# Gate and up loop of a two-layer trunk: where loads and sums for the down projection are written

## The chip, the cores and the metric

The kernel runs on one core of one Trainium2 chip. The metric is the time of one execution on the device in microseconds, as the median of repeated runs. The profile shows a single execution, taken by the hardware profiler; its engines are TensorE (PE, and PEld for its weight loads), VectorE (DVE), ScalarE (ACT), GpSimd (POOL) and SyncE (SP, which issues the DMAs).

## The reference, cut to what matters

Two residual layers, each with a token mixer and a dense SwiGLU block, in float32 on 1024 tokens of width 1024. The change touches the second half of each layer alone:

```python
def swiglu(h, w_gate, w_up, w_down):
    return (jax.nn.silu(h @ w_gate) * (h @ w_up)) @ w_down

for layer in range(DEPTH):
    ...
    hn = rms_norm(h, norm_ffn_g[layer])
    h = h + swiglu(hn, ffn_w_gate[layer], ffn_w_up[layer], ffn_w_down[layer])
return rms_norm(h, norm_final_g)
```

The hidden width is 2816, that is 22 tiles of 128.

## The kernel before, in words

Every matrix product is made of three products of parts: each float32 operand is split into a high part and a rest (`split`, lines 99 to 102: ScalarE copies the high part in line 101, VectorE subtracts it in line 102), and `mm3` (lines 122 to 127) sums high x high, high x rest and rest x high. The tokens stand in two halves of 512. Gate and up projections of one tile f are multiplied together as a 2 x 2 block product with seven block products instead of eight, after Strassen and Winograd; so is the down projection that follows. That is why there are sums and differences of weights and of activations everywhere.

`Up.run` (lines 429 to 455) is the gate and up loop. `turn` does tiles 0 to 2 with an order written out by hand; from f = 3 to 21 a loop follows, in which the order on each engine is up to the planner of the framework: what stands earlier in the program goes first, among the instructions that are ready in the planner's own model of time. Engines and SyncE's queue then work strictly in the order planned. One iteration loads and prepares the weights of tile f (`weights`, lines 314 to 321, with `sums`, `part_c` and `part_d` on GpSimd in lines 296, 297, 307 and 311), and does seven products of twelve matmuls: `p1` and `p2`, then the last two of the tile before in `end` (lines 377 to 391), then `p6`, `p5` and `p7`. Of these lines the text below needs:

- `snap` (line 339): ScalarE copies the first product once in each iteration. `add11` (line 343) and `gate11` (line 346) make the gate of the first half of tokens.
- `p6` copies its sum out on ScalarE in line 366, and `p7` goes on summing into the same accumulator, so TensorE's seventh product waits for that copy. `p7` makes the copy of line 371 and the add of line 372.
- `end`: line 381 makes the gated tile of the first half of tokens (`h0`), and line 382 stores it. Line 387 (VectorE), line 388 (ScalarE) and line 389 (GpSimd, in place) make that of the second half (`h1`), and line 390 stores it.

The down projection reads combinations of gated tiles and of weights, which this loop prepares beside its products:

- `combine` (lines 394 to 409). For f under 11, the first half: VectorE makes h1 - h0 into a scratch tile (line 399), which line 400 stores to `ts[0, f]`. For f from 11 on, the second half: lines 402 and 404 load `ts[0, f - 11]` and `hid[1, f - 11]` into scratch tiles, VectorE makes three differences (lines 405 to 407), and line 409 stores them. It is written at the end of iteration f + 1.
- `sums_down` (lines 411 to 421). The down weights of a layer are summed in 22 blocks: line 415 loads a block into the only tile `sd` of 128 x 4 x 256, lines 416 to 419 make four sums in place on VectorE, line 420 stores the tile. The call at the end of an iteration does as many blocks as are due there, one in most, two in a few.

The scratch tiles (`kl`, line 352) are six, shared by the gate, the copy of line 371 and the tiles of `combine`. The gated tiles (`hid`) are four, two for each f. All DMAs of this part are issued on SyncE's queue.

Of the kernel before, what the change touches and what calls it, by code (L numbers as in the profile page):

```python
# [9 lines left out]
F32 = mybir.dt.float32  # L10
# [6 lines left out]
MULT, ADD, SUB, MAX, MIN = ALU.mult, ALU.add, ALU.subtract, ALU.max, ALU.min  # L17

P = 128
# [8 lines left out]
NF = 22  # L28
KH = KT // 2
ND = 4 * (NF // 2) * P  # L30
SB = 256
# [23 lines left out]
def hybrid_trunk_kernel(ctx: ExitStack, tc: tile.TileContext, x_t, w_all, w_down, w_ba, vecs, c_f, c_i, c_rope, out):  # L55
    nc = tc.nc
    V, S, G, T = nc.vector, nc.scalar, nc.gpsimd, nc.tensor
    dma = nc.sync.dma_start
# [30 lines left out]
    def psg():  # L89
        return ps.tile([P, HT], F32, tag="g", name="psg", bufs=2)  # L90
# [4 lines left out]
    def psm():  # L95
        return ps.tile([P, HT], F32, tag="m", name="psm", bufs=3)
# [50 lines left out]
    class Trunk:  # L147
        def __init__(self, es):
            self.hp = es.enter_context(pool("trunk", side="right"))
            self.short = es.enter_context(ExitStack())  # L150
            self.p = self.short.enter_context(pool("tmp", side="right"))
            self.h = {}
            self.acc, self.sq = {}, {}
# [98 lines left out]
    class Up:  # L252

        def __init__(self, layer, left):
            self.layer, self.left, self.n = layer, left, 0
            self.hid = dr.tile([NH, NF, P, HT], F32, name=f"hid{layer}")
            self.ts = dr.tile([4, NF // 2, P, HT], F32, name=f"ts{layer}")
            self.sums_d = dr.tile([4, P, ND], F32, name=f"sd{layer}")
            self.tiles, self.blocks = {}, 0
            self.units = {f: {} for f in range(NF)}  # L260
            self.x, self.y, self.z, self.u2, self.g1, self.c22 = {}, {}, {}, {}, {}, {}
            self.snaps = self.right = None
            self.loads = 0
# [113 lines left out]
        def end(self, f, t4, b22):  # L377
            x, z = self.x.pop(f), self.z.pop(f)
            self.prod(x, f, "a22", t4, first=False)
            h = self.first.pop() if self.first else self.hidden()  # L380
            V.tensor_tensor(h, self.g1.pop(f), x, op=MULT)
            dma(self.hid[0, f], h)
            self.tiles[f] = [h]
            self.prod(z, f, "s4", b22, first=False)
            del self.units[f]
            h = self.hidden()
            V.tensor_tensor(h, self.u2.pop(f), z, op=ADD)
            S.activation(h, h, AF.Silu)  # L388
            G.tensor_tensor(h, h, self.c22.pop(f), op=MULT)  # L389
            dma(self.hid[1, f], h)  # L390
            self.tiles[f].append(h)


        def combine(self, f):
            h0, h1 = self.tiles.pop(f)
            g = f - NF // 2
            t = self.scratch("td")
            if g < 0:
                V.tensor_tensor(t, h1, h0, op=SUB)
                dma(self.ts[0, f], t)  # L400
                return
            dma(t, self.ts[0, g])
            t3, t4 = self.scratch("td"), self.scratch("td")
            dma(t3, self.hid[1, g])
            V.tensor_tensor(t, h1, t, op=SUB)
            V.tensor_tensor(t3, h1, t3, op=SUB)
            V.tensor_tensor(t4, h0, t, op=SUB)
            for i, x in enumerate((t, t3, t4)):
                dma(self.ts[i + 1, g], x)

        def sums_down(self, upto):
            while self.blocks < upto:
                c = slice(self.blocks * SB, (self.blocks + 1) * SB)
                a = self.right.tile([P, 4, SB], F32, tag="sd", name="sd", bufs=1)
                dma(a, w_down[self.layer].rearrange("x y p n -> p (x y) n")[:, :, c])
                V.tensor_tensor(a[:, 3], a[:, 2], a[:, 3], op=ADD)  # L416
                V.tensor_tensor(a[:, 2], a[:, 0], a[:, 2], op=SUB)
                V.tensor_tensor(a[:, 0], a[:, 3], a[:, 0], op=SUB)
                V.tensor_tensor(a[:, 1], a[:, 1], a[:, 0], op=SUB)
                dma(self.sums_d.rearrange("s p n -> p s n")[:, :, c], a)  # L420
                self.blocks += 1

        def prepared(self, f, src, left, right, u=None):
# [5 lines left out]
        def run(self, tr, row, b11, b21, hx, close, left, right):  # L429

            E = mybir.EngineType
            with tc.manual_schedule(engines={E.PE, E.DVE, E.Activation, E.Pool}):
                b22, t3, t4 = self.turn(tr, row, b11, b21, hx, close, left, right)
            t1, t2 = self.t12
            self.weights(3)
            self.p7(2, t3)
            for f in range(3, NF):
                if f > 3:
                    self.weights(f)
                self.p1(f, b11)  # L440
                self.p2(f, b21, psm())
                g = self.snap(f)
                if f == 3:
                    self.combine(0)
                    self.combine(1)
                self.end(f - 1, t4, b22)
                self.add11(f, g)
                self.gate11(f)
                self.p6(f, t2)
                self.p5(f, t1, psg())  # L450
                self.p7(f, t3)
                self.combine(f - 1)
                self.sums_down((f - 2) * (ND // SB) // (NF - 3))
            self.end(NF - 1, t4, b22)
            self.combine(NF - 1)

        def turn(self, tr, row, b11, b21, hx, close, left, right):

# [780 lines left out]
    def mixer_cd(hn, hp, second, close):  # L1239
# [6 lines left out]
        with ExitStack() as es:  # L1246
# [298 lines left out]
            class Attend:  # L1545
# [37 lines left out]
                def outputs(self, n):  # L1583
                    pt = self.pt.pop(n)
                    if n % 2 == 0:
                        self.po = psm()
                    po = self.po
                    for j, jj, m, z in self.blocks(n):
                        for i in range(m):
                            T.matmul(po[:, jj * P:(jj + 1) * P], pt[:, z.start + i * P:z.start + (i + 1) * P],  # L1590
                                     self.vp[:, j - m + 1 + i, :], start=i == 0, stop=i == m - 1)
                    if n % 2 == 0:
                        return
                    h, p, g = self.h, self.p, n // 2
                    ol = tl("ol", (4, 132), 2)
                    S.copy(ol[:, :, 0:P], po.rearrange("p (j d) -> p j d", j=4))
                    w = P + 2
                    sums = self.st[:, 4 * g:4 * g + 4, :]
                    if p == 0:
                        late.append(combine(h, g, ol, sums))  # L1600
                        next(late[-1])
                        return
                    V.tensor_copy(ol[:, :, P:w], sums)
                    if p == 1:
                        o4 = ol.rearrange("i (r b) d -> i b r d", b=2)
                        d4 = scr_o[h, 0].rearrange("(b i r) d -> i b r d", b=2, r=4)
# [351 lines left out]
```

## Time and profile before

| what | us |
| --- | --- |
| median of 3 runs | 2673.35 (2670.13 to 2674.11) |
| the profiled execution's own time | 2670.03 |
| its span in the profile | 2668.3 |
| PE busy | 2608.6 (98%) |
| DVE busy | 1658.3 (62%) |
| ACT busy | 1007.3 (38%) |
| POOL busy | 476.5 (18%) |

The gate and up loop of layer 0 lies at about 563 to 963 us of the span, that of layer 1 at about 2033 to 2435. In a row of the timeline stand the start, the length, engine and line, the operation, what it writes and reads with its shape, and in brackets how long the engine was idle before it and what it then waited for. In a row of the groups stand the count, busy time and mean in ns, and the idle time before. In a row of the waits stand who waited for whom, the total, how many times, and the longest.

### The profile page before, as it was taken

Reading aid. Unit: us, or ns where it says so; the run is one execution under the profiler, and the core shown is the slowest. Engines: PE = TensorE matmul, PEld = TensorE weight load, DVE = VectorE, ACT = ScalarE, POOL = GpSimd, SP = SyncE. Lnnn points to the kernel's source line nnn. Section 1 sums busy time; section 2 is a strip of 40 time slices with the busy share of each in tenths; the row PEclk is TensorE's granted clock in tenths of the full one; section 3 lists DMA queues with packets and bytes.
Section 4 is the critical chain, followed back from the end, with each engine's and each line's share of the span. In section 5 each row is a group of like instructions: output and inputs, shape, how many; then the busy total and the mean of one; then the engine's idle time right before and its main releaser. Section 6 shows DMA issues by size and latency. Waiting matters only on the chain.

```text
span 2668.3 us, 37189 instructions
## 1 busy us (share of the span) xinstructions
PE 2608.6 (98%) x14307; PEld 2173.6 (81%) x14307; DVE 1658.3 (62%) x2784; ACT 1007.3 (38%) x1655; POOL 476.5 (18%) x434
## 2 busy tenths in 40 slices
PE   8999999989999999999999999999999999999998
PEld 6888888877778878888888888888887777888887
DVE  7887676685556555554665557477658555655554
ACT  4432123343233344333444344454434222334442
POOL 1110111343334300010000000000033333330001
PEclk9999999999999999999999999999999999999999
DMA  4425447335665488641222322324743556547853
GB/s 139 141 90 169 118 133 247 105 115 174 194 200 182 150 267 281 187 148 60 80 65 68 91 61 68 99 65 126 251 136 115 170 182 196 199 146 255 279 172 119
DMA packets 239698, 402.96 MB, mean 151 GB/s; under 512 B 30081, under 2 KB 114593, under 8 KB 239393
## 3 DMA queue, kind: packets, MB, share of 16 engines
q1 hardware_dynamic: 239520, 400.59, 46.3%
q8 instruction: 112, 1.84, 0.3%
q14 instruction: 66, 0.53, 0.1%
HBM read 280.36 MB, written 120.14 MB: 150 GB/s over the span
## 4 chain that ended last, share of the span: by engine, by line
PE 52%; DMA 6%; DVE 4%; issue 1%; POOL 1%; ACT 0%; SPq 0%; DVEq 0%; POOLq 0%; ACTq 0%
PE psu L125 11%; PE psu L127 11%; PE psu L126 11%; DMA sd<-in_dram 3%; PE psm L127 2%; PE psm L125 2%; PE psm L126 2%; DMA sd<-sd 2%; PE psg L125 2%; PE psg L127 2%; PE psg L126 2%; PE psm L1590 1%; PE psm L1564 1%; DVE w L102 1%; PE psg L1353 1%
## 5 line engine op out<-in xcount | busy, mean ns | idle before, releaser
L125 PE MATMUL psu<-hnh,w 128*128 128x512 f32 x1328 | 530.3, 399 | 7.5 <-ACT w L101 7.5
L127 PE MATMUL psu<-hnh,w 128*128 128x512 f32 x1328 | 519.4, 391 | 0.0
L126 PE MATMUL psu<-hnl,w 128*128 128x512 f32 x1328 | 518.5, 390 | 0.0
L102 DVE TENSOR_TENSOR w<-raw,w 128x1024 fp32r<-128x1024 f32 (+1 forms) x316 | 387.7, 1228 | 190.7 <-ACT w L101 189.6
L101 ACT CAST w<-raw 128x1024 fp32r<-128x1024 f32 (+1 forms) x316 | 307.4, 976 | 394.8 <-PE psu L127 134.1
L125 PEld LDWEIGHTS psu<-hnh,w 128*128 128x128 f32 x1328 | 250.5, 189 | 57.8 <-ACT w L101 7.5
L127 PEld LDWEIGHTS psu<-hnh,w 128*128 128x128 f32 x1328 | 249.6, 188 | 54.2 <-DVE w L102 0.8
L126 PEld LDWEIGHTS psu<-hnl,w 128*128 128x128 f32 x1328 | 250.3, 188 | 50.1 <-DVE hnl L1749 0.5
L186 POOL TENSOR_TENSOR acc<-acc,sq 128x512 f32<-128x512 f32 x48 | 70.5, 1468 | 514.4 <-ACT sq L182 514.4
L102 DVE TENSOR_TENSOR hidq<-hr,hidq 128x1024 fp32r<-128x1024 f32 x84 | 95.3, 1135 | 86.8 <-ACT hidq L101 86.5
L416 DVE TENSOR_TENSOR sd<-sd 128x256 f32<-128x256 f32 x44 | 24.6, 560 | 187.9 <-DMA sd<-in_dram 171.7
L101 ACT CAST hidq<-hr 128x1024 fp32r<-128x1024 f32 x84 | 82.2, 980 | 122.5 <-DMA hr<-ts 56.9
L125 PE MATMUL psu<-w,hnh 128*128 128x512 f32 (+1 forms) x320 | 113.1, 353 | 0.0
L127 PE MATMUL psu<-w,hnl 128*128 128x512 f32 (+1 forms) x320 | 111.2, 347 | 0.0
L126 PE MATMUL psu<-w,hnh 128*128 128x512 f32 (+1 forms) x320 | 111.1, 347 | 0.0
L125 PE MATMUL psu<-t3h,w 128*128 128x512 f32 x176 | 75.6, 429 | 34.7 <-ACT u L366 34.7
L311 POOL TENSOR_TENSOR raw<-raw,ws 128x512 f32<-128x512 f32 x38 | 51.1, 1344 | 308.5 <-DVE w L102 308.5
L125 PE MATMUL psm<-hidq,w 128*128 128x512 f32 (+1 forms) x275 | 106.0, 385 | 0.0
L126 PE MATMUL psm<-hidq,w 128*128 128x512 f32 (+1 forms) x275 | 105.8, 385 | 0.0
L127 PE MATMUL psm<-hidq,w 128*128 128x512 f32 (+1 forms) x275 | 105.8, 385 | 0.0
L389 POOL TENSOR_TENSOR hid<-hid,c 128x512 f32<-128x512 f32 x44 | 79.6, 1808 | 128.1 <-ACT hid L388 99.6
L1391 POOL COPY attn<-ac 32x128 f32<-32x128 f32 x32 | 13.3, 416 | 434.6 <-DVE ac L1357 381.7
(429 smaller groups left out, 5807.6 us busy)
## 6 DMA issues: line engine op xcount, KB each, us to landing
raw<-in_dram SPq DMA_DIRECT2D x228, 512.0 KB, 4.0
sd<-in_dram SPq DMA_DIRECT2D x44, 512.0 KB, 4.0
hid<-hid SPq DMA_DIRECT2D x88, 256.0 KB, 2.3
sd<-sd SPq DMA_DIRECT2D x44, 512.0 KB, 3.0
ts<-td SPq DMA_DIRECT2D x88, 256.0 KB, 2.2
hr<-ts SPq DMA_DIRECT2D x40, 512.0 KB, 4.1
raw<-sd SPq DMA_DIRECT2D x40, 512.0 KB, 4.1
hr<-hid SPq DMA_DIRECT2D x30, 512.0 KB, 4.5
```

What stands on the lines that cost most here:

```text
L101: S.copy(hi, src)
L102: eng.tensor_tensor(lo, src, hi.bitcast(F32), op=SUB)
L125: T.matmul(o, lh, rh, start=first and i == 0, stop=False, **kw)
L126: T.matmul(o, lh, rl, start=False, stop=False, **kw)
L127: T.matmul(o, ll, rh, start=False, stop=last and i == n - 1, **kw)
L186: (eng or G).tensor_tensor(a, a, q, op=ADD)
L311: G.tensor_tensor(a[:, HT:], a[:, HT:], s[:, :HT], op=SUB)
L389: G.tensor_tensor(h, h, self.c22.pop(f), op=MULT)
L416: V.tensor_tensor(a[:, 3], a[:, 2], a[:, 3], op=ADD)
L1353: T.matmul(od[r * 32:(r + 1) * 32, c * 32:(c + 1) * 32], a[:, z], x[:, z], start=True, stop=True, tile_position=(0, r * 32))
L1564: T.matmul(o[:, z], self.q[:, j * P:(j + 1) * P], self.k[:, (j - m + 1) * P:(j + 1) * P], start=True, stop=True)
L1590: T.matmul(po[:, jj * P:(jj + 1) * P], pt[:, z.start + i * P:z.start + (i + 1) * P], self.vp[:, j - m + 1 + i, :], start=i == 0, stop=i == ...
```

## The change

`combine` is taken apart. The first half of a tile f under 11 is now made at the end of `end`, on GpSimd, in place in the first gated tile. The second half is two calls: `ask` loads its two tiles, and is written after `p6` and before `p5` of the next iteration; `second_half` makes the differences after `p7`, where `combine` was, and puts the third into the first gated tile instead of a third scratch tile. `sums_down` now sums and stores the block that the call before it loaded, and then loads the next one; it is called once in every iteration at its end, and at f = 6, 10, 14 and 18 also before `p5`. The two `combine` calls for tiles 0 and 1 at f = 3 go, since `end` does them. The products, their order and the weights' preparation stay.

```diff
             dma(self.hid[1, f], h)
             self.tiles[f].append(h)
+            if f < NF // 2:
+                self.first_half(f)
...
-        def combine(self, f):
+        def first_half(self, f):
             h0, h1 = self.tiles.pop(f)
-            g = f - NF // 2
-            t = self.scratch("td")
-            if g < 0:
-                V.tensor_tensor(t, h1, h0, op=SUB)
-                dma(self.ts[0, f], t)
-                return
-            dma(t, self.ts[0, g])
-            t3, t4 = self.scratch("td"), self.scratch("td")
-            dma(t3, self.hid[1, g])
-            V.tensor_tensor(t, h1, t, op=SUB)
-            V.tensor_tensor(t3, h1, t3, op=SUB)
-            V.tensor_tensor(t4, h0, t, op=SUB)
-            for i, x in enumerate((t, t3, t4)):
-                dma(self.ts[i + 1, g], x)
-
-        def sums_down(self, upto):
-            while self.blocks < upto:
-                c = slice(self.blocks * SB, (self.blocks + 1) * SB)
-                a = self.right.tile([P, 4, SB], F32, tag="sd", name="sd", bufs=1)
-                dma(a, w_down[self.layer].rearrange("x y p n -> p (x y) n")[:, :, c])
+            G.tensor_tensor(h0, h1, h0, op=SUB)
+            dma(self.ts[0, f], h0)
+
+        def ask(self, f):
+            if f in self.tiles:
+                t2, t3 = self.scratch("t2d"), self.scratch("t3d")
+                dma(t2, self.ts[0, f - NF // 2])
+                dma(t3, self.hid[1, f - NF // 2])
+                self.tiles[f] += [t2, t3]
+
+        def second_half(self, f):
+            if f in self.tiles:
+                h0, h1, t2, t3 = self.tiles.pop(f)
+                V.tensor_tensor(t2, h1, t2, op=SUB)
+                V.tensor_tensor(t3, h1, t3, op=SUB)
+                V.tensor_tensor(h0, h0, t2, op=SUB)
+                for i, x in enumerate((t2, t3, h0)):
+                    dma(self.ts[i + 1, f - NF // 2], x)
+
+        def sums_down(self, more=True):
+            if self.block:
+                c, a = self.block
                 V.tensor_tensor(a[:, 3], a[:, 2], a[:, 3], op=ADD)
                 V.tensor_tensor(a[:, 2], a[:, 0], a[:, 2], op=SUB)
                 V.tensor_tensor(a[:, 0], a[:, 3], a[:, 0], op=SUB)
                 V.tensor_tensor(a[:, 1], a[:, 1], a[:, 0], op=SUB)
                 dma(self.sums_d.rearrange("s p n -> p s n")[:, :, c], a)
+            self.block = None
+            if more and self.blocks < ND // SB:
+                c = slice(self.blocks * SB, (self.blocks + 1) * SB)
+                a = self.right.tile([P, 4, SB], F32, tag="sd", name="sd", bufs=1)
+                dma(a, w_down[self.layer].rearrange("x y p n -> p (x y) n")[:, :, c])
+                self.block = c, a
                 self.blocks += 1
...
                 g = self.snap(f)
-                if f == 3:
-                    self.combine(0)
-                    self.combine(1)
                 self.end(f - 1, t4, b22)
                 self.add11(f, g)
                 self.gate11(f)
                 self.p6(f, t2)
+                self.ask(f - 1)
+                if f in (6, 10, 14, 18):
+                    self.sums_down()
                 self.p5(f, t1, psg())
                 self.p7(f, t3)
-                self.combine(f - 1)
-                self.sums_down((f - 2) * (ND // SB) // (NF - 3))
+                self.second_half(f - 1)
+                self.sums_down()
             self.end(NF - 1, t4, b22)
-            self.combine(NF - 1)
+            self.ask(NF - 1)
+            self.second_half(NF - 1)
+            self.sums_down(False)
```

More of the change, by code (lines that the diff above doesn't have):

```diff
@@ L258, in __init__ @@
             self.sums_d = dr.tile([4, P, ND], F32, name=f"sd{layer}")
-            self.tiles, self.blocks = {}, 0
+            self.tiles, self.blocks, self.block = {}, 0, None
             self.units = {f: {} for f in range(NF)}
```

## The prediction

> **What bounds the kernel now.** TensorE is the engine that is never short of work, so I read first where it waits in the gate and up loops, by the busy time in stretches: layer 0 while the blocks of the down weights are summed (563 to 820), and after that (820 to 963). Columns: length, then each engine's busy time, then the granted clock.
>
> ```profile
> 563.00:820.00 257.00, 240.32 (x1020) 195.01 (x1019) 152.83 (x212) 82.16 (x116) 91.80 (x64) 0.97 0.59 190
> 820.00:963.00 143.00, 143.00 (x633) 118.41 (x632) 76.81 (x86) 54.09 (x73) 47.68 (x33) 1.00 0.50 169
> ```
>
> In the second stretch TensorE is busy 143.00 of 143.00 us: nothing there can be gained. In the first it is idle for 16.7 us and its clock is 0.97. The copy of line 339 runs once in each iteration, so it is a clock for the loop (layer 0 with blocks, layer 0 without, layer 1 with; count, and first and last start):
>
> ```profile
> L339 ACT COPY gt<-psu x12: 587/587/589, 581.7 to 814.0; 128x512 f32<-128x512 f32 x12
> ...
> L339 ACT COPY gt<-psu x7: 580/587/588, 833.1 to 948.0; 128x512 f32<-128x512 f32 x7
> ...
> L339 ACT COPY gt<-psu x12: 587/588/591, 2051.7 to 2286.6; 128x512 f32<-128x512 f32 x12
> ```
>
> With blocks an iteration takes 232.3 / 11 = 21.12 us in layer 0 and 234.9 / 11 = 21.35 us in layer 1; without, 114.9 / 6 = 19.15 us. The loss is 11 x 1.97 + 11 x 2.20 = 46 us. That is all this change can win in the loops.
>
> Who causes it? The waits in the first stretch (total, times, longest), and then one iteration on VectorE, SyncE's queue, ScalarE and TensorE:
>
> ```profile
> DVE sd L416 <- DMA sd<-in_dram: 78.3, 19, 7.7
> ...
> PE psu L125 <- ACT u L366: 15.8, 7, 5.1
> ```
>
> ```profile
> 686.42 1.40 DVE L417 TENSOR_TENSOR sd<-sd 128x256 f32<-128x256 f32 x1
> 687.85 1.40 DVE L418 TENSOR_TENSOR sd<-sd 128x256 f32<-128x256 f32 x1
> 689.29 0.42 DVE L419 TENSOR_TENSOR sd<-sd 128x256 f32<-128x256 f32 x1
> 689.63 0.69 DVE L102 TENSOR_TENSOR w<-raw,w 128x512 fp32r<-128x512 f32 x1
> 690.23 0.68 DVE L399 TENSOR_TENSOR td<-hid 128x512 f32<-128x512 f32 x1
> 690.83 0.68 DVE L372 TENSOR_TENSOR c<-c,psg 128x512 f32<-128x512 f32 x1
> 696.81 0.42 DVE L416 TENSOR_TENSOR sd<-sd 128x256 f32<-128x256 f32 x1 [5.29 <-DMA sd<-in_dram]
> ...
> 698.53 0.68 DVE L343 TENSOR_TENSOR gt<-gt,psm 128x512 f32<-128x512 f32 x1
> ...
> 702.79 0.67 DVE L387 TENSOR_TENSOR hid<-u,psg 128x512 f32<-128x512 f32 x1
> ```
>
> ```profile
> 689.74 0.37 SPq L420 DMA_DIRECT2D sd<-sd  x1
> 690.34 0.33 SPq L269 DMA_DIRECT2D raw<-in_dram  x1
> 692.76 0.38 SPq L415 DMA_DIRECT2D sd<-in_dram  x1
> 693.19 0.51 SPq L400 DMA_DIRECT2D ts<-td  x1
> ```
>
> ```profile
> 703.50 0.63 ACT L388 ACTIVATE hid<-hid 128x512 f32<-128x512 f32 x1 [1.73 <-DVE hid L387]
> 704.04 0.57 ACT L366 COPY u<-psu 128x512 f32<-128x512 f32 x1
> ```
>
> ```profile
> 704.66 0.79 PE L125 MATMUL psu<-t3h,w 128*128 128x512 f32 x1 [2.31 <-ACT u L366]
> 705.25 0.63 PE L126 MATMUL psu<-t3l,w 128*128 128x512 f32 x1
> ```
>
> Read them as one chain. The old block's sums end at 689.7, its store goes at 689.74, and the only buffer is free when that has landed; the next load goes at 692.76 and lands 4 us later, at 696.8. VectorE, which takes its work in order, stands for 5.29 us, and behind it stand the adds of lines 343 and 387; behind 387 the activation of line 388, behind that the copy of line 366, and for that copy TensorE waits 2.31 us and then runs at a lower clock (0.63 us a matmul). The loop with blocks is thus **bound by a round trip**, sums, store, load, that goes twice in an iteration.
>
> Is the block late because it is asked for late in the program? The loads of layer 1:
>
> ```profile
> L415 SPq DMA_DIRECT2D sd<-in_dram x22: 379/383/445, 2033.0 to 2283.0; - x22
> ```
>
> The program puts the last of 22 loads behind the last iteration (f = 21). It went at 2283.0, and the twelfth copy of line 339 (f = 14) was at 2286.6. So the planner that orders the program takes a block as soon as its buffer is free in its own reckoning, and runs seven iterations ahead of the text. Where the call stands in the text hardly matters.
>
> **The change, part by part.** The sum is made against the profiled execution: 2670.03 us, of which 2668.3 are the span. The median of the three times is 2673.35, 3.3 us more, and I add the sum to that.
>
> *Blocks: load written before the other half of the iteration, sums at the next call.* Flattened, the sequence before and after is the same: load, four sums, store, load. There is still one buffer, so no load can pass the store before it. The planner already issues each as soon as it may; I take 0 us. The bounds: the whole 46 us if placement does count (a rival below), and 10 us lost if the sums, now of a later rank, are each put off by half a microsecond (about one 0.42 us sum) in 22 iterations.
>
> *First halves on GpSimd.* These leave VectorE and come to GpSimd; the nearest row there is line 389, also in place on two such tiles:
>
> ```profile
> L416 DVE TENSOR_TENSOR sd<-sd 128x256 f32<-128x256 f32 x22 | 12.7, 579 | 92.6 <-DMA sd<-in_dram 78.3 <-issue 14.3
> ...
> L399 DVE TENSOR_TENSOR td<-hid 128x512 f32<-128x512 f32 x11 | 9.0, 827 | 0.0
> ```
>
> ```profile
> L389 POOL TENSOR_TENSOR hid<-hid,c 128x512 f32<-128x512 f32 x13 | 22.5, 1729 | 24.9 <-ACT hid L388 24.9
> ```
>
> VectorE loses 2 x 9.0 = 18 us of work. But in the iteration above line 399 stands between the block's store and the wait for the next load; what VectorE saves there it waits longer. I count 0 (the other end: all 18 us won, if it stood ahead of the sums each time). GpSimd gains 22 x 1.73 = 38 us, and was busy 91.8 of 257 us, so it has room for it. It has a price beside VectorE, though: the sums of 686.42 and 687.85 took 1.40 us instead of 0.42, while GpSimd ran this:
>
> ```profile
> 687.49 1.48 POOL L307 TENSOR_TENSOR raw<-raw 128x512 f32<-128x512 f32 x1
> ```
>
> The mean of line 416 is 0.579, so 0.15 us above 0.42 for a sum, at 91.8 us of GpSimd work; 88 sums in a layer give 13 us. Eight first halves in the stretch (f = 3 to 10) add 13.8 us to the 91.8, 15%, so 2 us a layer, and 4 in all. Since the round trip is the bound, I count them in full: **+4 us** (from 0 if they fall into idle time of VectorE, to 16 x 0.98 = 16 if each hits one sum).
>
> The Trainium skill, page "SBUF — State Buffer", section "Who interferes with whom", says that a VectorE instruction with two inputs in SBUF contends with a GpSimd instruction that reads SBUF, and that the loser blocks for the whole instruction. The 1.40 us beside GpSimd's 1.48 agree with that; by it the term goes to its upper end, and speaks against this edit.
>
> The difference goes into the first tile itself, so GpSimd must wait until that tile's own store (line 382) has been read, and the tile is held until the difference has landed. Line 381, which makes it, stands ahead of line 387 on VectorE; from 387's start at 702.79 to the activation's end at 704.13 and through line 389's 1.73 us are 3.1 us, and the block's store, twice as large, landed in 692.76 - 689.74 = 3.0 us. Four tiles for two in an iteration leave the tile a whole iteration more. I take 0 us; if that cover is gone, up to 3.0 us in an iteration that it hits. Behind the first half on GpSimd stand the weight differences of the next tile (lines 296 to 311); with GpSimd busy 91.8 of 257 us they have the room, 0 us, and 1.73 us where they are late.
>
> Line 400's store now waits for GpSimd, and SyncE's queue runs in order. Behind it can stand a block's store or load. The two in the closest case:
>
> ```profile
> 624.14 0.33 SPq L390 DMA_DIRECT2D hid<-hid  x1
> 624.56 0.39 SPq L420 DMA_DIRECT2D sd<-sd  x1
> ```
>
> Line 390 waits for GpSimd's product. With line 400 between these two, the block's store would go 1.73 - 0.42 = 1.3 us later; above, 4.9 us separate the product's end (684.86) from the store (689.74), and nothing is lost. From 0 to 16 x 1.3 = 21 us; I take 0, for the planner sees that store ready later than now and the last row of the SyncE fence has it behind the load.
>
> *Second halves: the two loads asked for before the fifth product.* They free VectorE of this wait, in both layers (total, times, longest):
>
> ```profile
> DVE td L405 <- DMA td<-ts: 41.2, 16, 6.0
> ```
>
> Most of it lies after the last block, where TensorE had no idle time (143.00 of 143.00): 0 us. Second halves begin at f = 12 and the blocks reach to f = 14, so one or two in a layer lie beside blocks, at 41.2 / 16 = 2.6 us; of at most 10 us I take 2, since TensorE waited for a fifth as long as VectorE in the first stretch (15.8 of 78.3). The loads pass the block's load and the weights' in SyncE's queue, and hold two of six scratch tiles half an iteration longer; with the third difference written in place of the other tile, three scratch tiles become two. Cost 0 to 4 us, taken as 0.
>
> *The loop's end.* The last `end` waits once, here in layer 0:
>
> ```profile
> 966.47 0.50 PE L125 MATMUL psu<-t4h,w 128*128 128x512 f32 x1 [2.04 <-ACT c L371]
> ```
>
> The moved loads may make that 2 us better or worse in each layer; 0. The sum: 0 + 4 - 2 = +2 us, so 2675 us.
>
> **The rivals.** *Placement counts (0.16).* If the planner does follow the text, the load comes half an iteration, some 9 us, before its sums: more than the 4 us it needs, and only 23 calls over 19 iterations. VectorE's wait is gone, and iterations fall from 21.2 to 19.15: -46, 2627 us (2617 to 2645). Against it speaks the row of line 415; for it, that the wait is as large as it is.
>
> *The planner re-sorts, to the good (0.19).* Without line 399, and with the second halves ready sooner, the planner deals VectorE's order anew, and in part of the iterations the blocks fall behind line 387 and not ahead of line 343. Each iteration that is freed gives 46 / 22 = 2.1 us; for eight of 22 that is 17: 2656 us (2645 to 2668).
>
> *GpSimd gets in the way (0.20), slower.* The first half's store stands ahead of the block's store in SyncE's queue, and its run beside the block's sums. Price 1.3 us for the queue or 0.98 for a sum, in each of 16 iterations, about 19 together: 2692 us (2680 to 2705). It decides the sign from about five iterations on (5 x 1.3 = 6.5). For it: at 624 a store that waits for GpSimd already stands right ahead of the block's. Against it: the room on GpSimd.
>
> The Trainium skill, page "GPSIMD Engine Reference", section "4.1 Engine selection", advises against GpSimd for elementwise work on two inputs, as about twice as slow; 1.73 against 0.83 us agree. By that page alone this rival is the likeliest.
>
> **How the numbers follow.** My forecast has 0.45, and its own range is 2664 to 2681. Under 0.2% (5.3 us either way), about what a measurement of this kernel can tell from no change, lie 0.28 of it, faster 0.05, slower 0.12. Faster in all: 0.05 + 0.16 + 0.19 = 0.40; same 0.28; slower 0.12 + 0.20 = 0.32. The range for 8 in 10 leaves out half of the first rival below (0.08) and the last one's upper end and a little more above (0.10): 2628 to 2695.
>
> **What would show it.** If I am right, the 22 loads of a layer's blocks still run to about f = 14, VectorE's wait at the first sum of a block stays near 78 us in the stretch of layer 0, and line 339 keeps about 21 us in an iteration with blocks. The first halves show on GpSimd near 1.5 us, and the second halves' wait for their loads is nearly gone with no gain. I am wrong if the blocks spread over all iterations, or if the round trip from one block's store to the next block's first sum is much off 7 us.

## The result, and the profile after

| | median, us | lowest to highest | runs |
| --- | --- | --- | --- |
| before | 2666.67 | 2663.59 to 2674.11 | 19 |
| after | 2676.38 | 2674.51 to 2681.51 | 19 |

The ratio is 1.0034, with a 95% interval of 1.0027 to 1.0041: the change makes the kernel **slower by 0.34%**, 9.7 us. The profiled execution of after took 2675.43 us, of which 2673.7 are the span; that of before 2670.03 and 2668.3. Before's profiled execution lies 3.4 us above its median, after's 1.0 below, so the two traces show only 5.4 of the 9.7 us.

First the stretch with blocks (length, busy time of PE, PEld, DVE, ACT and POOL, granted clock, DMA share, GB/s), then line 339 as the clock of the loop (layer 0 with blocks, without, layer 1 with), in the kernel after:

```profile
563.00:828.00 265.00, 241.72 (x1023) 195.83 (x1022) 154.95 (x200) 81.75 (x115) 110.00 (x75) 0.96 0.56 186
```

```profile
L339 ACT COPY gt<-psu x12: 587/587/591, 582.3 to 821.7; 128x512 f32<-128x512 f32 x12
...
L339 ACT COPY gt<-psu x7: 580/587/589, 840.7 to 955.7; 128x512 f32<-128x512 f32 x7
...
L339 ACT COPY gt<-psu x12: 587/587/589, 2055.7 to 2292.9; 128x512 f32<-128x512 f32 x12
```

An iteration with blocks now takes 239.4 / 11 = 21.76 us in layer 0 and 237.2 / 11 = 21.56 us in layer 1; without, 115.0 / 6 = 19.17 us as before. The loss against 19.17 has gone from 46 to 28.5 + 26.3 = 55 us. So the iterations with blocks take some 9 us longer in this trace. About 4 of these come back outside them (the wait of 2.04 us at the end of layer 0's loop is gone, and so is one of 1.53 us in layer 1), which leaves the 5.4 us between the two traces. VectorE's wait for blocks has not gone (waits in that stretch; loads of blocks in layer 1):

```profile
DVE sd L421 <- DMA sd<-in_dram: 85.2, 19, 8.2
...
PE psu L125 <- ACT u L366: 22.4, 10, 8.2
```

```profile
L430 SPq DMA_DIRECT2D sd<-in_dram x22: 368/383/426, 2037.3 to 2294.2; - x22
```

VectorE waits 85.2 us for blocks (78.3 before), TensorE 22.4 us for the copy of line 366 (15.8 before). The last of 22 loads goes at 2294.2, beside the twelfth copy of line 339 (f = 14): the planner runs ahead of the text as it did.

Then the two engines between which work was moved, in the iteration that the prediction read (f = 7), VectorE and GpSimd:

```profile
687.59 0.51 DVE L421 TENSOR_TENSOR sd<-sd 128x256 f32<-128x256 f32 x1 [2.26 <-issue]
688.13 1.40 DVE L422 TENSOR_TENSOR sd<-sd 128x256 f32<-128x256 f32 x1
689.57 1.40 DVE L423 TENSOR_TENSOR sd<-sd 128x256 f32<-128x256 f32 x1
691.00 1.40 DVE L424 TENSOR_TENSOR sd<-sd 128x256 f32<-128x256 f32 x1
```

```profile
686.54 1.27 POOL L399 TENSOR_TENSOR hid<-hid 128x512 f32<-128x512 f32 x1
687.77 1.48 POOL L296 TENSOR_TENSOR ws<-raw 128x512 f32<-128x512 f32 x1
689.33 1.36 POOL L297 TENSOR_TENSOR ws<-ws,raw 128x512 f32<-128x512 f32 x1
690.65 1.47 POOL L307 TENSOR_TENSOR raw<-raw 128x512 f32<-128x512 f32 x1
```

Line 399 is the first half. Here it pushes the weight differences behind it (lines 296, 297, 307) 1.3 us later, so that they now cover three of the four sums and not two: the fourth takes 1.40 us, where before it took 0.42. In other iterations it runs beside a sum itself. Worked out from the starts and lengths of both engines' timelines in layer 0: 7.0 of line 399's 17.9 us lie beside a block's sums, and 17 of 88 sums take over 0.8 us, where 12 did before. Over both layers, the four sums of a block before and after (count, busy, mean ns, idle before):

```profile
L416 DVE TENSOR_TENSOR sd<-sd 128x256 f32<-128x256 f32 x44 | 24.6, 560 | 187.9 <-DMA sd<-in_dram 171.7 <-issue 16.2
L419 DVE TENSOR_TENSOR sd<-sd 128x256 f32<-128x256 f32 x44 | 24.0, 546 | 1.2
L418 DVE TENSOR_TENSOR sd<-sd 128x256 f32<-128x256 f32 x44 | 23.5, 534 | 1.2
...
L417 DVE TENSOR_TENSOR sd<-sd 128x256 f32<-128x256 f32 x44 | 22.4, 509 | 0.9
```

```profile
L422 DVE TENSOR_TENSOR sd<-sd 128x256 f32<-128x256 f32 x44 | 32.9, 748 | 1.1
L424 DVE TENSOR_TENSOR sd<-sd 128x256 f32<-128x256 f32 x44 | 27.6, 628 | 1.3
L423 DVE TENSOR_TENSOR sd<-sd 128x256 f32<-128x256 f32 x44 | 26.4, 601 | 1.2
...
L421 DVE TENSOR_TENSOR sd<-sd 128x256 f32<-128x256 f32 x44 | 22.0, 500 | 173.0 <-DMA sd<-in_dram 168.8 <-issue 4.2
```

Together 94.5 us before and 108.9 after, 14.4 us more. Last, the place where the loop begins (f = 3). SyncE's queue, before and then after:

```profile
584.99 0.38 SPq L269 DMA_DIRECT2D raw<-in_dram  x1
```

```profile
575.85 0.40 SPq L425 DMA_DIRECT2D sd<-sd  x1
...
587.78 0.32 SPq L400 DMA_DIRECT2D ts<-hid  x1
588.19 0.38 SPq L269 DMA_DIRECT2D raw<-in_dram  x1
588.67 0.40 SPq L430 DMA_DIRECT2D sd<-in_dram  x1
```

VectorE there, after, and TensorE, before and then after:

```profile
594.71 1.22 DVE L102 TENSOR_TENSOR w<-ws,w 128x1024 fp32r<-128x1024 f32 x1 [9.52 <-ACT w L101]
```

```profile
598.07 0.80 PE L125 MATMUL psu<-t3h,w 128*128 128x512 f32 x1 [5.08 <-ACT u L366]
```

```profile
601.86 0.79 PE L125 MATMUL psu<-t3h,w 128*128 128x512 f32 x1 [8.23 <-ACT u L366]
```

The first half's store (587.78) waits for GpSimd. Behind it in the queue stand a load of weights (line 269) and the second block's load (588.67), though the tile of that block had long been free: the first block's store went at 575.85. Before, these two loads went at 584.99 and 585.43, ahead of the first halves' stores. What comes last here is the weights: line 297 on GpSimd waits for them, line 101 for line 297, and VectorE in line 102 for line 101; the sums and line 387 stand behind that. TensorE's wait grows from 5.08 to 8.23 us.

So there were two candidates for the loss. **Theory C**: GpSimd's new work lengthens the sums of the blocks beside it. **Theory Q**: the first half's store, which waits for GpSimd, stands ahead of loads in SyncE's queue, a block's among them. And one question behind both: is the loop really bound by the round trip through one tile, as the prediction says, so that only a shorter round trip helps?

### The profile page after: what moved, and what is told of

It is laid out like the page before. It is cut to its first block, busy times and chain, and to the rows that moved or that the text cites. A ratio compares the mean times of both kernels' runs of the same rounds, so it can differ in the third digit from the quotient of the medians.

```text
span 2673.7 us, 37198 instructions
## 1 busy us (share of the span) xinstructions
PE 2606.6 (97%) x14307; PEld 2173.0 (81%) x14307; DVE 1670.0 (62%) x2762; ACT 1005.5 (38%) x1655; POOL 517.7 (19%) x456
## 4 chain that ended last, share of the span: by engine, by line
PE 74%; DMA 12%; DVE 10%; issue 2%; POOL 2%; ACT 1%; SPq 0%; DVEq 0%; POOLq 0%; ACTq 0%
PE psu L125 16%; PE psu L127 15%; PE psu L126 15%; DMA sd<-in_dram 5%; DMA sd<-sd 5%; PE psg L125 3%; PE psg L127 3%; PE psg L126 3%; PE psm L126 3%; PE psm L127 3%; PE psm L125 3%; DVE sd L422 1%; DVE w L102 1%; PE psm L1603 1%; PE psm L1577 1%
```

## The experiments

| run | median, us | before beside it | ratio (95%) |
| --- | --- | --- | --- |
| e1_first | 2676.08 | 2667.09 | 1.0034 (1.0021 to 1.0046) |
| e3_ask | 2672.37 | 2667.09 | 1.0018 (1.0009 to 1.0027) |
| e8_late | 2675.30 | 2667.09 | 1.0033 (1.0021 to 1.0046) |
| e4_vec | 2661.26 | 2667.22 | 0.9980 (0.9969 to 0.9991) |
| e9_double | 2680.86 | 2667.22 | 1.0060 (1.0048 to 1.0073) |
| e12_memset | 2676.82 | 2666.50 | 1.0042 (1.0028 to 1.0056) |
| e5_two | 2709.68 | 2667.22 | 1.0160 (1.0146 to 1.0174) |
| e6_tied | 2615.80 | 2667.09 | 0.9810 (0.9796 to 0.9823) |
| e10_load | 2630.91 | 2666.50 | 0.9865 (0.9851 to 0.9879) |
| e11_sum | 2616.41 | 2666.50 | 0.9811 (0.9797 to 0.9825) |
| e7_tied | 2617.79 | 2667.22 | 0.9820 (0.9807 to 0.9833) |
| e13_tied_vec | 2615.99 | 2666.50 | 0.9808 (0.9794 to 0.9822) |

**The parts of the change.** The block edit, put into the kernel before by itself, gives the same program, instruction for instruction and in the same order on all five engines. It got no run for that reason; its effect is zero by construction. The other two parts were run alone.

*e1_first: the kernel before, with the first halves on GpSimd in place.*

```diff
             self.tiles[f].append(h)
+            if f < NF // 2:
+                self.first_half(f)
...
+        def first_half(self, f):
+            h0, h1 = self.tiles.pop(f)
+            G.tensor_tensor(h0, h1, h0, op=SUB)
+            dma(self.ts[0, f], h0)
...
         def combine(self, f):
+            if f not in self.tiles:
+                return
...
-                if f == 3:
-                    self.combine(0)
-                    self.combine(1)
```

> The kernel before with one part of the change: the first halves made on GpSimd, in place, at the end of end; second halves and blocks as before. Theory Q (the first half's store now waits for GpSimd in SyncE's queue, ahead of the weights' loads and of the block's store and load): nearly all of the loss, 2673 to 2678 us against 2666.7 before, and line-339 iterations with blocks near 21.5 us. Theory C (GpSimd's extra work slows the block's sums on VectorE): the same time, so this run only tells the part. Rival L (the loads asked for early are what costs): 2665 to 2669.

It costs 9.0 us alone, nearly as much as the whole change.

*e3_ask: the kernel before, with the second halves' loads asked for half an iteration ahead and the third difference in place; first halves stay on VectorE.*

```diff
+        def ask(self, f):
+            if f >= NF // 2:
+                t2, t3 = self.scratch("t2d"), self.scratch("t3d")
+                dma(t2, self.ts[0, f - NF // 2])
+                dma(t3, self.hid[1, f - NF // 2])
+                self.tiles[f] += [t2, t3]
...
                 self.p6(f, t2)
+                self.ask(f - 1)
...
+            self.ask(NF - 1)
             self.combine(NF - 1)
```

> The kernel before with the other part: the second halves' loads asked for before the fifth product, the third difference in place; first halves stay on VectorE, blocks as before. Q and C: 2664 to 2669 us, nothing lost, and VectorE's waits for these loads (41.2 us before) nearly gone. L: 2673 to 2678.

A miss: nothing was to be lost by it, and it is 5.3 us slower, just short of the range of rival L. Its trace shows a gain and a loss side by side. TensorE's busy time and matmuls (x) where the blocks end and behind it, before and then in this run:

```profile
790.00:850.00 60.00, 59.99 (x265) 1.00 0.60 203
850.00:980.00 130.00, 127.96 (x557) 0.99 0.55 186
```

```profile
790.00:850.00 60.00, 56.72 (x242) 0.97 0.58 200
850.00:980.00 130.00, 130.00 (x575) 1.00 0.56 192
```

Behind the blocks TensorE does 18 matmuls more: the wait at the loop's end is gone. But where the last blocks lie it does 23 fewer. SyncE's queue there, then VectorE and TensorE, in this run:

```profile
798.33 0.43 SPq L427 DMA_DIRECT2D sd<-sd  x1
...
804.03 0.38 SPq L422 DMA_DIRECT2D sd<-in_dram  x1
...
810.86 0.38 SPq L427 DMA_DIRECT2D sd<-sd  x1
...
819.38 0.32 SPq L416 DMA_DIRECT2D ts<-hid  x1
819.75 0.43 SPq L422 DMA_DIRECT2D sd<-in_dram  x1
```

```profile
807.54 0.43 DVE L423 TENSOR_TENSOR sd<-sd 128x256 f32<-128x256 f32 x1 [4.25 <-DMA sd<-in_dram]
```

```profile
812.62 0.67 PE L125 MATMUL psu<-t3h,w 128*128 128x512 f32 x1 [2.67 <-ACT u L366]
```

The last block's load (819.75) follows its predecessor's store by 8.9 us, where 4.8 us lay between them before (4.0 us on average, 21 pairs in before's layer 0): the second half's three stores now stand ahead of it in the queue, and each waits for a difference on VectorE. But TensorE's wait lies ahead of that load, and the iteration behind it takes 19.0 us, as without blocks. The wait hangs on the block before: its load (804.03) follows a store by 5.7 us, and VectorE stood 4.25 us for it, ahead of line 387. In the kernel before that block's load went at 796.75, and its sums waited 0.23 us. The second half's differences got longer too, because they now start as soon as line 389 ends and run beside GpSimd's weight differences (the first of three, both layers, before and e3_ask):

```profile
L405 DVE TENSOR_TENSOR td<-hid,td 128x512 f32<-128x512 f32 x22 | 15.4, 700 | 42.4 <-DMA td<-ts 41.2 <-POOL hid L389 1.2
```

```profile
L412 DVE TENSOR_TENSOR t2d<-hid,t2d 128x512 f32<-128x512 f32 x22 | 21.6, 984 | 23.6 <-POOL hid L389 23.6
```

This reading is of one profile, whose span differs from before's by only 0.6 us (both executions lie off their medians in opposite senses); why the block before the last comes later, by the queue, by VectorE's order or by the longer differences, no run took asunder. By the medians the parts don't add up either: 9.0 + 5.3 = 14.3 us alone, 9.7 together, at the edge of what the intervals allow.

**Theory Q by itself.** *e8_late: the kernel after, with each first half's store tied in SyncE's queue behind a block's load, so that the load no longer waits for GpSimd.*

```diff
-            dma(self.ts[0, f], h0)
+            self.firsts.append(dma(self.ts[0, f], h0))
...
-                dma(a, w_down[self.layer].rearrange("x y p n -> p (x y) n")[:, :, c])
+                self.block_loads.append(dma(a, w_down[self.layer].rearrange("x y p n -> p (x y) n")[:, :, c]))
...
+            for t, n in zip(self.firsts, (1, 1, 2, 4, 6, 8, 10, 12, 14, 16, 18)):
+                tc.add_manual_dep(t.ins, self.block_loads[n].ins.name, mybir.DependencyInfo(
+                    mybir.DependencyClass.NoSync, mybir.DependencyReason.DATA), reason="order")
```

> The changed kernel with one thing moved: each first half's store stands behind the next block load in SyncE's queue, as in the kernel before; GpSimd still makes the difference, in place. Q: the loss goes, 2665 to 2670 us, and block loads wait for the block's own store again. C: it stays, 2673 to 2678.

The queue is mended at the loop's start, and TensorE's waits there and one iteration on are, in after, the 8.23 us shown above and the row of the first fence; in e8_late the two rows of the second:

```profile
623.77 0.50 PE L125 MATMUL psu<-t3h,w 128*128 128x512 f32 x1 [0.62 <-ACT u L366]
```

```profile
598.93 0.79 PE L125 MATMUL psu<-t3h,w 128*128 128x512 f32 x1 [6.32 <-ACT u L367]
623.70 0.79 PE L125 MATMUL psu<-t3h,w 128*128 128x512 f32 x1 [3.47 <-ACT u L367]
```

The block's load goes 2.4 us earlier (at 586.28, for 588.67), the wait at f = 3 falls by 1.9 us, and at f = 4 comes back 2.9 us larger. The time doesn't move: to mend the queue in this way gains nothing. It does not rule Theory Q out, since the planner also dealt VectorE's order anew, and the table below shows this run losing at the loop's start what it wins later.

**Theory C by itself.** *e4_vec: the kernel after, the first half in place on VectorE.*

```diff
-            G.tensor_tensor(h0, h1, h0, op=SUB)
+            V.tensor_tensor(h0, h1, h0, op=SUB)
```

> The changed kernel with the first half made on VectorE, in place, at the same point of the program; its store keeps its place in SyncE's queue, right behind line 390's store and ahead of the block's store and next load. Theory C (GpSimd's extra work slows the block's sums on VectorE and so the round trip): 2664 to 2670 us, and the sums' means back from about 0.62 to about 0.54 us. Theory Q (the store's place in the queue): 2673 to 2678.

Faster than C expected, and faster than before. The sums are shorter (the four means in layer 0 are 571, 557, 425 and 425 ns, 1.98 us together; before 2.17, after 2.47; 6 of 88 take over 0.8 us). But the planner also deals the order anew: here the second block's load goes at 578.36, ahead of the second first half's store, and not at 588.67. So the run has two causes in it and cannot price C by itself.

*e9_double and e12_memset: the kernel after with more GpSimd work behind each first half: the same difference once more into a scratch tile that nothing reads, or two fills of such a tile. Both have after's order on VectorE and SyncE.*

```diff
             G.tensor_tensor(h0, h1, h0, op=SUB)
+            G.tensor_tensor(self.scratch("again"), h1, h0, op=SUB)
```

```diff
             G.tensor_tensor(h0, h1, h0, op=SUB)
+            again = self.scratch("again")
+            for _ in range(2):
+                G.memset(again, 0.0)
```

> The changed kernel with GpSimd's first half doubled: the same difference once more into a scratch tile that nothing reads; the queue's order is that of the change, and no store waits for the second. C: as much again as the first cost, 2682 to 2688 us, and the sums' means near 0.7 us. Q: 2675 to 2679.

> The changed kernel with two fills of a scratch tile on GpSimd behind each first half, in the place of the doubled difference of e9_double; the order on VectorE and in SyncE's queue is that of the change. If GpSimd hurts because its reads of SBUF hold up VectorE's sums (Trainium skill, page SBUF — State Buffer, section Who interferes with whom: an instruction that only writes does not contend with two-input ones): 2674 to 2678 us, as the change, and the sums' means unchanged. If it hurts because its own next work comes later: 2680 to 2685, as e9_double.

The third and fourth sum of a block in layer 0, in e9_double (after has 601 and 628 ns there too):

```profile
L424 DVE TENSOR_TENSOR sd<-sd 128x256 f32<-128x256 f32 x22 | 16.1, 733 | 0.6
L425 DVE TENSOR_TENSOR sd<-sd 128x256 f32<-128x256 f32 x22 | 15.8, 716 | 0.7
```

and in e12_memset:

```profile
L427 DVE TENSOR_TENSOR sd<-sd 128x256 f32<-128x256 f32 x22 | 13.8, 629 | 0.7
L426 DVE TENSOR_TENSOR sd<-sd 128x256 f32<-128x256 f32 x22 | 13.2, 601 | 0.6
```

A second difference lengthens the sums again (22 of 88 over 0.8 us) and costs some 4.5 us over after, between what Q and what C expected; all five runs lie above all five of e12_memset, though the two intervals overlap. The fills leave the sums at after's 601 and 629 ns, and the time's interval overlaps after's. The order on VectorE and SyncE is the same in all three, so neither order nor GpSimd's busy time makes the difference, but what of its work lies beside the sums: by the timelines 9.5 of the second difference's 15.2 us do. A rival is that the second difference makes GpSimd's weight differences later. The fills don't test it, since the planner put most of them behind the weight differences (1.3 of 11.6 us beside sums); but VectorE's wait for weights (line 102 for line 101, layer 0 with blocks) does not grow, 15.5 us in e9_double for 16.1 in after. **C is shown as a cause**, with its sign and rough size. Whether a fill that does lie beside a sum is harmless these runs hardly tell. In each layer one sum starts beside a fill alone; in layer 0 it starts at 612.41, and the two fills run from 611.55 for 1.11 us. Here is VectorE there, the sum ahead of it beside GpSimd's line 307 (610.32, for 1.29 us):

```profile
610.40 1.49 DVE L424 TENSOR_TENSOR sd<-sd 128x256 f32<-128x256 f32 x1 [7.08 <-DMA sd<-in_dram]
...
612.41 0.41 DVE L425 TENSOR_TENSOR sd<-sd 128x256 f32<-128x256 f32 x1
```

The one beside the difference takes 1.49 us, the one that starts beside the fill 0.41. The Trainium skill, page "SBUF — State Buffer", section "Who interferes with whom", says that a VectorE instruction with two SBUF inputs contends with a GpSimd instruction that reads SBUF, not with one that only writes. The differences agree: in before's trace the 143 sums with no GpSimd instruction beside them take 0.41 to 0.43 us each, the other 33 take 1.03 us on average. For the fill two sums agree, of 0.41 us each.

**Where the time lies.** The starts of line 339's copies divide the iterations with blocks into three parts. In us, both layers together, one execution of each kernel (so a difference of 2 or 3 us means little):

| run | first four (f = 3 to 6) | next six (f = 7 to 12) | last (f = 13) | all eleven |
| --- | --- | --- | --- | --- |
| before | 173.2 | 254.3 | 39.7 | 467.3 |
| after | 171.3 | 259.5 | 45.7 | 476.6 |
| e1_first | 171.3 | 260.1 | 41.7 | 473.1 |
| e3_ask | 174.1 | 251.5 | 45.9 | 471.5 |
| e8_late | 179.6 | 251.9 | 48.9 | 480.4 |
| e4_vec | 163.8 | 252.9 | 43.3 | 460.0 |
| e9_double | 174.1 | 264.8 | 44.3 | 483.2 |
| e12_memset | 172.9 | 258.4 | 48.1 | 479.3 |

The loss of after sits in two places, and each part of the change run alone has one of them. In the next six iterations after loses 5.2 us and e1_first 5.8: there the blocks' sums take 60.5 us in after for 51.1 before, while the way from a block's store to the next load is as long as it was (3.6 us on average for 3.5), so this part came with C and not with Q. e9_double loses 5.3 us more there, e12_memset nothing. In the last iteration after loses 6.0 us and e3_ask 6.2. The longer wait at f = 3 is given back: the first four iterations together are no longer than before. Of e4_vec's lead over after, 7.5 us lie in the first four, where the second block's load goes so much earlier, and 6.6 in the next six. e8_late loses 8.3 us against after in the first four and wins 7.6 in the next six, with sums nearly as long as after's (59.6 us) and a shorter way from store to load (3.0 us): what C costs there, a shorter way in the queue can win back.

**Is the round trip the bound?** *e5_two: the kernel before with blocks of half the size in two tiles, so that one can be loaded while the other is summed.*

```diff
-SB = 256
+SB = 128
...
-                a = self.right.tile([P, 4, SB], F32, tag="sd", name="sd", bufs=1)
+                a = self.right.tile([P, 4, SB], F32, tag="sd", name="sd", bufs=2)
```

> The kernel before with 44 blocks of half the size in two tiles, so that one block's load goes while the other's sums and store do; nothing is tied. If the round trip through one tile is the bound: 2625 to 2650 us. If the planner then only takes blocks faster and VectorE waits for each: 2660 to 2680.

Both expectations missed: it is 1.6% slower. The waits of its first stretch:

```profile
DVE sd L416 <- DMA sd<-in_dram: 63.4, 25, 6.3
...
PE psu L125 <- ACT u L366: 30.3, 9, 5.9
```

VectorE waits less for blocks (63.4 us, 78.3 before), TensorE twice as long for line 366's copy (30.3, 15.8 before). A second tile, with blocks of half the size, doesn't free the loop: the planner takes more in an iteration instead (in layer 0 as much as 2.2 whole blocks on average, for 1.9 before). The other way is to take fewer.

*e6_tied: the kernel before with the block edit of the change and two ties that only order, without a semaphore: a block's load behind the store of line 390 last written, its first sum behind the add of line 343 or 372 last written. e11_sum has the second tie alone, e10_load the first.*

```diff
-            V.tensor_tensor(g, g, self.y.pop(f), op=ADD)
+            self.on_v = V.tensor_tensor(g, g, self.y.pop(f), op=ADD)
...
-            V.tensor_tensor(c, c, self.z[f], op=ADD)
+            self.on_v = V.tensor_tensor(c, c, self.z[f], op=ADD)
...
-            dma(self.hid[1, f], h)
+            self.on_sp = dma(self.hid[1, f], h)
...
+        def behind(self, ins, other):
+            tc.add_manual_dep(ins.ins, other.ins.name, mybir.DependencyInfo(
+                mybir.DependencyClass.NoSync, mybir.DependencyReason.DATA), reason="pace")
...
-                V.tensor_tensor(a[:, 3], a[:, 2], a[:, 3], op=ADD)
+                self.behind(V.tensor_tensor(a[:, 3], a[:, 2], a[:, 3], op=ADD), self.on_v)
...
-                dma(a, w_down[self.layer].rearrange("x y p n -> p (x y) n")[:, :, c])
+                self.behind(dma(a, w_down[self.layer].rearrange("x y p n -> p (x y) n")[:, :, c]), self.on_sp)
```

> The kernel before, with the blocks split as in the change (sums at the call after the load) and held to their place in the program: a block's load may not go ahead of the last store of line 390 written before it in SyncE's queue, its first sum not ahead of the last add of line 343 or 372 written before it on VectorE. If the planner's running ahead makes a round trip of two blocks an iteration the bound: blocks spread to f = 21, iterations near 19.2 us throughout, 2620 to 2640 us. If VectorE's waits for the loads cost by themselves, wherever the blocks stand: 2655 us or more.

> As e6_tied, but only the block's load is held to its place in the program; the sums go where the planner puts them. If the pace of the loads alone is what matters: 2614 to 2622 us, as e6_tied. If VectorE must also not be given the sums too early: 2625 to 2655, with VectorE's waits for the loads mostly left.

> As e6_tied, but only the block's first sum is held to its place on VectorE; the load may go as soon as the tile is free. Since the tile comes free only behind the sums, the pace should be the same and the load has the longest start: 2612 to 2618 us. If the loads must be held too: above 2625.

In e6_tied, the stretch with blocks, line 339 over the whole loop, and the waits for blocks:

```profile
563.00:820.00 257.00, 255.66 (x1128) 211.62 (x1127) 161.98 (x193) 93.28 (x128) 106.56 (x71) 1.00 0.52 173
```

```profile
L339 ACT COPY gt<-psu x19: 578/587/590, 579.4 to 923.5; 128x512 f32<-128x512 f32 x19
```

```profile
DVE sd L418 <- DMA sd<-in_dram: 12.2, 4, 3.8
...
PE psu L125 <- ACT u L366: 1.3, 1, 1.3
```

TensorE is busy 255.66 of 257 us; an iteration takes 344.1 / 18 = 19.12 us throughout, as without blocks. 51 us are won, with the same one tile, the same transfers and the same sums; only the pace is different. e11_sum, one edge for each block, gives the same within the intervals, and e10_load most of it. There a block comes no faster than it is used, but its sums stand too early on VectorE; over both layers (171.7 us, 40 times, before):

```profile
DVE sd L418 <- DMA sd<-in_dram: 102.9, 39, 6.4
```

*e7_tied and e13_tied_vec: the kernel after with the two ties of e6_tied (first diff), and the same with the first half on VectorE as well (second).*

```diff
+                self.behind(V.tensor_tensor(a[:, 3], a[:, 2], a[:, 3], op=ADD), self.on_v)
...
+                self.behind(dma(a, w_down[self.layer].rearrange("x y p n -> p (x y) n")[:, :, c]), self.on_sp)
```

```diff
-            G.tensor_tensor(h0, h1, h0, op=SUB)
+            V.tensor_tensor(h0, h1, h0, op=SUB)
```

> The changed kernel with the blocks held to their place in the program, as in e6_tied. If the round trip of the blocks is what lets GpSimd's work and the moved stores reach TensorE: 2612 to 2620 us, as e6_tied. If they cost TensorE on their own: 2623 or more.

> The changed kernel with the blocks held to their place as in e7_tied, and the first half on VectorE as in e4_vec. Theory C with the round trip as the bound: with that gone the engine of the first half hardly matters, 2613 to 2619 us. If GpSimd's work costs on its own: 2 us or more below e7_tied's 2617.8.

As expected. Once the blocks are paced, GpSimd or VectorE for the first halves makes no difference that can be measured (2617.79 and 2615.99 us, intervals overlapping), and the change as a whole costs 2 us against e6_tied by the medians, intervals overlapping too. The sums are no shorter for it (layer 0: 56.0 us in e6_tied and 56.9 in e7_tied, 47.7 before, 54.3 after): they cost time where main work stands behind them on VectorE. The best versions are e6_tied, e11_sum and e13_tied_vec, alike at 1.9% below before.

## Why the prediction was right and wrong

The time forecast, 2675 us, lies 1.4 us from the result, but for a reason that deserves no trust: it added +2 to the median of three runs, 2673.35, and over 19 runs that median is 2666.67. The forecast of the *change* was +2, and +9.7 came: more than its own bound of 5.3 us for "the same", half way to the rival "GpSimd gets in the way" (+19). Point by point:

- **The planner runs ahead; the block edit is worth 0.** Right, and exactly so: the order is identical.
- **First halves on GpSimd, +4.** The mechanism was right, the size wrong: e1_first costs 9.0 us. The step that failed scaled the 13 us of a layer's lengthened sums by GpSimd's busy time: 15% more work, 15% more lengthening. It counted eight first halves in the stretch, where its own row of line 399 has eleven, and it took line 416's mean for all four sums, which together took 47.7 us in layer 0, some 11 above 88 x 0.42. Above all, the new work is not spread like the old. By the timelines of layer 0, 14.5 of the 91.8 us of GpSimd's work before lay beside a block's sums, 16%; of line 399's it is 7.0 of 17.9, 39%, and it pushes other differences onto sums as well. The sums take 14.4 us more, near the upper end of 16 that was worked out and not chosen; 5 to 6 of them reach the end, by the next six iterations of after and e1_first.
- **VectorE's saved 18 us count 0.** Right, and more than that: VectorE is busier after than before (1670.0 for 1658.3 us), since the sums take 14.4 us more and the second halves' differences, at 984 ns for 700, some 19.
- **The difference in place, 0.** Right: GpSimd's line 399 waits for that tile's store 3 times and 2.3 us in all in the stretch of layer 0.
- **SyncE's queue, 0.** Near enough in its sum, wrong in its reason. It was costed at nothing because the planner would see the store ready late and set it behind the load; the planner set it ahead. At the loop's start that delays a load of weights and a block's load by 3.2 us each, and TensorE's wait grows as much; the next iterations give it back.
- **Second halves, -2.** The sign was wrong: e3_ask is 5.3 us slower, and after has the same loss in its last iteration with blocks. The wait for their loads is gone (41.2 to nothing) as forecast, and what is late next is line 389 (23.6 to 28.5 us). The step that failed costed the place of the moved DMAs in the queue at 0 to 4 us and took it as 0: with them a block's load came later, and VectorE stood for it ahead of line 387. That their place alone does it is not shown.
- **"Bound by a round trip."** Half right. The round trip sets the time *because* VectorE, in order, is committed to two blocks in an iteration with their sums ahead of lines 343 and 387. With the same round trip, ties alone win 51 us, and a second, smaller tile without ties loses 43. The 46 us that the prediction called all there was to win were there, and no edit of this change reached for them.

Open: what of the moved loads, their stores and the longer differences makes the last iteration with blocks lose 6 us; how much C and how much the new order is worth in e4_vec, one word away from after and 15 us faster; and how the two layers' losses shift from one iteration to the next.

## What to carry to other kernels

When an ordering planner places side work that is fed by DMA, and an in-order engine stands waiting for it in front of main work, moving the calls in the text can leave the order wholly as it was; look at the order first. An order-only edge that holds the side work to the pace of the main loop won 1.9% here, where another buffer, earlier loads and another engine won nothing. And when work goes to GpSimd, count beside which two-input sums of VectorE it, and what it pushes, will run, not its share of GpSimd's time.

## What the runs showed of the hardware

- A VectorE sum of 128 x 256 takes 0.42 us alone and 1.40 us beside a GpSimd difference of two tiles (1.27 to 1.48 us), and the second halves' differences of 128 x 512 went from 700 to 984 ns on average when they came to lie beside GpSimd's.
- A store that waits for GpSimd or VectorE holds back the loads behind it in SyncE's queue although their tile is free: 12.8 us from the first block's store to the second's load at the loop's start (10.2 before, behind the store of line 390), 8.9 us at the last block of e3_ask (4.8 before), against 4.0 on average.
- A wait of TensorE can cost more than its length. Behind the 2.31 us at 704.66 in the kernel before, the granted clock was 0.50 from 704.6 to 707.5, and a matmul took 0.63 us for 0.39. In the two loops of before and after, no wait under 2.0 us was followed by such rows; of the longer ones most were, but not one of 3.47 us in after.
